# Reordering the beginning of a transformer-block kernel: tokens in column halves, modulation in chunks of 128 columns

## The chip, the cores and the metric

The kernel runs on one core of a Trainium2 chip. A core has five engines, each with its own in-order instruction stream: TensorE (PE in the profile; its weight loads are listed apart as PEld), VectorE (DVE), ScalarE (ACT), GpSimd (POOL) and SyncE (SP), which here only issues transfers. They share an on-chip memory of 128 partitions (SBUF); TensorE writes its results to accumulator banks (PSUM), of which this kernel uses eight, each of 128 x 512 fp32 values. The metric is device time in microseconds (us), the median of several runs; an arithmetic result in fp32 precision is wanted.

## The reference

One layer of a diffusion backbone, on 1024 latent tokens (a grid of 16 rows by 64 columns) and 256 context tokens of width 1024. What the change touches is its first two steps:

```
mod_x = silu(c) @ w_mod + b_mod                  # also for the context, with c_ctx
sh1, sc1, ... = split(mod_x, 6)
h_x = rmsnorm(x, g_pre_mix) * (1 + sc1) + sh1    # modulated tokens
u, q, k, v  = split(h_x @ w_in)                  # first 512 columns of w_in give u
```

After that come the pooling mixer, neighbourhood attention, an output projection and a squared-ReLU MLP. They are the same in both kernels.

## The kernel before, in words

**Precision.** A product of two fp32 matrices is made of three products in a faster format: each operand is split into a high part and the rest, a low part, and high x high, high x low and low x high are added up in one bank. ScalarE makes the high part (`high_part`, a rounding copy), VectorE the low part (`low_part`, a subtraction). For the weights w_in these are tiles `wu0h`, `wu0l` and so on, one pair for each 256 rows of K; for the tokens a page `hx`, whose first half is the high and whose second half the low part.

**The start.** All of it is recorded inside `in_order(...)`, which fixes the order of instructions on every engine to that of the program text. No scheduler moves anything: an instruction that waits holds up all that stands behind it on its engine.

1. SP issues the loads: eight tiles of 128 tokens (`token_tile`, 512 KB each), then for each of four quarters q of the columns the modulation weights (`mod_load`, four transfers of 512 KB, `wm`, which pick runs of 1 KB out of w_mod) and a weight block (`load`, 512 KB, `wu0w` to `wu3w`), then the context and further weights. At most eight transfers are outstanding: the ninth waits for the landing of the first, and so on.
2. Per token tile: ScalarE squares and sums (`mean_square`, L131), VectorE adds epsilon (L136, `vt_x`), POOL takes the inverse root (L140, `rt_x`), VectorE scales the tile (`normalised`, L334). In the program text the squares of tile n+1 and its epsilon add stand ahead of the scaling of tile n.
3. TensorE turns the scaled tiles (transposes, `turned`, L346) into PSUM banks `pxt`, 128 columns of K at a time, so that k = 0 to 7 counts chunks of 128 rows of K. `spare` (L341) fills with transposes of the identity. `by_bands` (L353) copies a bank to the page `xT[k]`, on ScalarE or VectorE, putting the tokens in the order of eight bands of 8 grid columns. Latent half b = 0 holds bands 0 to 3 and b = 1 bands 4 to 7, so each half needs all eight token tiles.
4. The modulation: for a quarter q, `mod_sums` (L401) makes 16 products of 256 columns with the activated vectors c and c_ctx as stationary operand, in four groups of 32 array columns; ScalarE copies the result (`mrow`, L406), two small products with a picking matrix (L418) turn it into columns, and VectorE makes scale a1 and shift s1 of two chunks k (`shift_scale`, L422 to L427).
5. `latent(b, k)` applies scale and shift to one half of chunk k and makes its high and low part: with `on_act` unset ScalarE writes the high part from xT (L208) and VectorE computes h again (L209) and subtracts (L210); with it set ScalarE computes h (L205), then the high part (L206).
6. `some_sums(b, js, k)` (L449) makes the wide products, 512 columns each, for output blocks js: 12 for b = 0 and four blocks, 6 for b = 1 and two.

The order before is: all eight tiles scaled and turned, first quarter of the modulation, then chunk by chunk the wide products, with the sums of the next quarter between them. Eight banks are shared: two of them (`lasting`) for the modulation and a few others, six for the rest.

Of the kernel before, what the change touches and what calls it, by code (L numbers as in the profile page):

```python
# [18 lines left out]
P = 128  # L19
# [5 lines left out]
GW = 64  # L25
# [44 lines left out]

def _pick_table():

    e = np.zeros((P, 4), np.float32)
    for w in range(2):
        for v in range(2):
            e[32 * w + v, 2 * w + v] = e[64 + 32 * w + v, 2 * w + v] = 1.0
    return e
# [3 lines left out]
def hybrid_block(ctx, tc, x, ctx_in, w_mod, b_mod, gp1, gp2, w_in, pool_w, rpb, w_out, w1, w2, vectors,  # L81
# [189 lines left out]
    with tc.tile_pool(name="ps1", bufs=6, space=PSUM) as ps1, tc.tile_pool(name="tmp1", bufs=3) as tmp:  # L271

        def bank(name):
            if name[:2] == "pm" or name in ("pxt1_0", "pxt0_2", "pxt1_7", "pct2", "pct3"):
                return lasting(name)
            return ps1.tile([P, 512], F32, tag="mm", name=name)
# [20 lines left out]
        def mod_load(q, kh, w):  # L297
            src = w_mod[:, w * D + q * 256 : w * D + (q + 1) * 256].rearrange("(h k p) f -> h p k f", p=P, h=2)
            t = page(f"wm{q}_{kh}_{w}")
            nc.sync.dma_start(t.rearrange("p (k f) -> p k f", k=4), src[kh])  # L300
            return t

        xn = [token_tile(f"x{n}", x[n * P : (n + 1) * P, :]) for n in range(NT)]
        wm, raw_u = [], []
        for q in range(4):
            wm.append([[mod_load(q, kh, w) for w in range(2)] for kh in range(2)])
            raw_u.append(load(f"wu{q}", pair(w_in, q, 0, 512)))
# [17 lines left out]
        inverse = {}  # L325

        def squares(name, t):
            jk = page(f"jk{name}")
            ms = sm(f"ms_{name}", 1, 4)
            mean_square(jk, t, ms)  # L330
            inverse[name] = rsqrt_of(f"t_{name}", ms)

        def normalised(name, t):
            nc.vector.tensor_scalar_mul(t, t, inverse[name])  # L334

        xT = [None] * KT

# [5 lines left out]
        def turned(pts, ns, ks):  # L343
            for k in ks:
                for n in ns:
                    nc.tensor.transpose(pts[k][:, (n % 4) * P : (n % 4 + 1) * P], xn[n][:, k * P : (k + 1) * P], ident)  # L346

        def by_bands(copy, h, ks):
            for k in ks:
                if xT[k] is None:  # L350
                    xT[k] = page(f"xT{k}")
                to = xT[k].rearrange("p (m r c) -> p m r c", m=NM, r=QR)[:, :, 8 * h : 8 * h + 8]
                copy(to, pts[h][k].rearrange("p (r m c) -> p m r c", m=NM, c=QC))  # L353


        on_act, on_dve = nc.scalar.copy, nc.vector.tensor_copy
        pts = [{}, {0: bank("pxt1_0")}]
        free = pts[1][0][:, 3 * P :]

        def turned_in(h, ns, ks):  # L360
            for k in ks:
                if k not in pts[h]:
                    pts[h][k] = bank(f"pxt{h}_{k}")
            turned(pts[h], ns, ks)

        spare(free, 30)
        squares("x0", xn[0])
        for n in range(NT):
            if n + 1 < NT:
                squares(f"x{n + 1}", xn[n + 1])  # L370
            if n == 5:
                by_bands(on_dve, 0, (0,))
            if n == 7:
                by_bands(on_dve, 0, (1,))
            normalised(f"x{n}", xn[n])
            if n < 4:
                turned_in(0, (n,), range(KT - 1))
        spare(free, 3)
        turned_in(1, (4,), (0,))
        spare(free, 10)  # L380
        turned_in(0, (0, 1, 2, 3), (7,))
        turned_in(1, (5,), (0,))
        spare(free, 3)
        by_bands(on_dve, 0, (2,))
        by_bands(on_act, 0, (3, 4, 5, 6, 7))
        turned_in(1, (4, 5), (4, 5))
        turned_in(1, (6,), (0, 4, 5))
        turned_in(1, (4, 5, 6), (1,))
        turned_in(1, (7,), (0, 1, 4, 5))
        turned_in(1, (4, 5, 6, 7), (6,))  # L390
# [5 lines left out]
        def mod_sums(q, pm, kh):  # L396
            for k in range(4 * kh, 4 * kh + 4):
                for w in range(2):
                    c = 2 * (k % 2) + w
                    o = (k % 4) * 256  # L400
                    nc.tensor.matmul(pm[32 * c : 32 * c + 32, :256], sT[:, k, :], wm[q][kh][w][:, o : o + 256],  # L401
                                     start=(k < 2), stop=(k >= KT - 2))

        def mod_kept(q, pm):
            mr = tmp.tile([P, 256], F32, tag="mrow", name=f"mrow{q}", bufs=2)
            nc.scalar.copy(mr, pm[:, :256])  # L406
            return mr
# [6 lines left out]

        def shift_scale(q, mr):
            pt = bank(f"pmt{q}")
            for j in range(2):
                nc.tensor.matmul(pt[:, 4 * j : 4 * j + 4], mr[:, j * P : (j + 1) * P], pck, start=True, stop=True)  # L418
            pv = pt[:, :8].rearrange("p (j w v) -> p w v j", w=2, v=2)
            hs = slice(2 * q, 2 * q + 2)  # L420
            for v in range(2):
                nc.vector.tensor_tensor(a1[v][:, hs], pv[:, 1, v], b_sc[:, hs], add)  # L422
                nc.vector.tensor_tensor(a1[v][:, hs], a1[v][:, hs], g1c[:, hs], mul)
                if q < 2:
                    nc.vector.tensor_tensor(s1[v][:, hs], pv[:, 0, v], b_sh[:, hs], add)
                else:
                    nc.vector.scalar_tensor_tensor(s1[v][:, hs], pv[:, 0, v], -1.0, b_sh[:, hs], mul, sub)  # L427
# [3 lines left out]
        def latent(b, k):  # L431
# [3 lines left out]
                      on_act=(b == 1), kept=src if b == 1 or k > 1 else None)  # L435
# [6 lines left out]
        pus = [[bank(f"pu{j}_{b}") for j in range(4 if b == 0 else 2)] for b in range(2)]  # L442

        def some_sums(b, js, k):
            h = hx[b][k]
# [17 lines left out]
        wu0h, wu0l = (whl.tile([P, 1024], F32R, tag="hl", name=f"wu0{n}") for n in "hl")  # L463
        by_bands(on_dve, 1, (0,))
        by_bands(on_act, 1, (1, 4, 5))
        by_bands(on_dve, 1, (6,))
        pm = bank("pm0")
        for kh in range(2):
            mod_sums(0, pm, kh)
        mr = mod_kept(0, pm)  # L470
        nc.scalar.copy(wu0h, raw_u[0])
        wgt.append((wu0h, wu0l))
        turned_in(1, (4, 5, 6, 7), (3,))
        shift_scale(0, mr)
        turned_in(1, (4, 5, 6, 7), (2, 7))
        nc.vector.tensor_tensor(wu0l, raw_u[0], wu0h.bitcast(F32), sub)
        latent(0, 0)
        latent(0, 1)
        by_bands(on_act, 1, (3, 2))
        by_bands(on_dve, 1, (7,))  # L480
        latent(1, 0)
        latent(1, 1)
        for q in range(4):
            some_sums(0, range(4), 2 * q)
            if q == 0:
                some_sums(0, (0, 1), 1)
            if q < 3:
                mr = mod_rows(q + 1)
                wgt.append(high_low(f"wu{q + 1}", raw_u[q + 1], 1.0 if q == 0 else -1.0))
            some_sums(0, range(2 if q == 0 else 0, 4), 2 * q + 1)  # L490
# [6 lines left out]
            if q == 2:  # L497
                for i, t in enumerate(cp):
                    squares(f"c{i}", t)
                for i, t in enumerate(cp):  # L500
                    normalised(f"c{i}", t)
# [46 lines left out]
        for k in range(2):  # L548
            hi, lo = hx[0][k][:, :512], hx[0][k][:, 512:]
# [1502 lines left out]
```

## Time and profile before

| | us |
|---|---|
| median of 3 runs (1027.5 to 1028.42) | 1027.59 |
| the profiled execution | 1028.11 |
| its span | 1026.3 |
| TensorE busy | 1012.1 |
| first wide product of the start | 23.18 |
| first product with the third weight block (wu2) | 45.01 |

Rows of a timeline give the start in us, the length in us, the engine, the line, the operation, out<-in, sizes and the count; in brackets the idle time of the engine before it and what ended it. Rows of waits give who waited for whom, us in total, times and the longest. Rows of a stretch give its length, then the busy time and the count for PE, PEld, DVE, ACT and POOL, the granted TensorE clock, the share of the transfer engines and GB/s. A matmul of fp32 operands shows as two records.

### The profile page before, as it was taken

The numbers are of one execution on the slowest core, as the hardware profiler recorded it, in microseconds if no ns is written. First come the engines' busy times: TensorE is split into PE (matmuls) and PEld (weight loads), VectorE is DVE, ScalarE is ACT, GpSimd is POOL, SyncE is SP. The second block draws the span as 40 slices with busy tenths as digits, with TensorE's granted clock in tenths as the row PEclk, the third lists the DMA queues.
The fourth block names the chain that finished last, engine by engine and source line by source line (L and its number), as shares of the span: only waits on it lengthen the run. The fifth ranks groups of instructions, "written<-read, shape, count | busy, mean of one in ns | idle before, by whom it ended". The sixth has DMA issues, their size and how long they took to land.

```text
span 1026.3 us, 16024 instructions
## 1 busy us (share of the span) xinstructions
PE 1012.1 (99%) x5910; PEld 839.0 (82%) x5910; DVE 746.8 (73%) x1156; ACT 546.0 (53%) x944; POOL 148.9 (15%) x230
## 2 busy tenths in 40 slices
PE   8999999999999999999999999999999999999997
PEld 6788888878898888888888888888888888888885
DVE  5588757977886688879998888755757666556576
ACT  7573254348896657776555554555543344334431
POOL 3011110156773321310000000000000000000001
PEclk9999999999999999999999999999999999999999
DMA  9999799623347966886776657537966766556556
GB/s 343 336 253 342 233 266 310 205 58 88 84 96 204 229 171 200 274 206 204 260 253 205 224 196 227 182 133 238 347 231 248 248 231 214 196 184 193 175 178 213
DMA packets 123134, 222.70 MB, mean 217 GB/s; under 512 B 9456, under 2 KB 55152, under 8 KB 123056
## 3 DMA queue, kind: packets, MB, share of 16 engines
q1 hardware_dynamic: 96560, 171.14, 50.7%
q0 software_dynamic: 9360, 19.58, 9.4%
q10 hardware_dynamic: 17136, 30.97, 8.1%
q8 instruction: 46, 0.75, 0.3%
q14 instruction: 32, 0.26, 0.1%
HBM read 168.16 MB, written 52.45 MB: 215 GB/s over the span
## 4 chain that ended last, share of the span: by engine, by line
PE 94%; DMA 2%; POOL 1%; ACT 1%; issue 1%; DVE 1%; SPq 0%; POOLq 0%; DVEq 0%; ACTq 0%
PE pu L449 4%; PE pa L1096 4%; PE phz L198 3%; PE phv L198 3%; PE pyx L198 3%; PE phx L198 3%; PE phx L200 3%; PE pyv L200 3%; PE pyx L200 3%; PE pyz L200 3%; PE pyv L199 3%; PE phz L199 3%; PE pyz L199 3%; PE phv L199 3%; PE phx L199 3%; PE phz L200 3%
## 5 line engine op out<-in xcount | busy, mean ns | idle before, releaser
L1042 ACT ACTIVATE sp<-sp,nm 128x640 f32<-128x640 f32 (+1 forms) x64 | 51.5, 805 | 9.6 <-DVE ri L1046 4.8
L1031 DVE CUSTOM_DVE_ANT_0 sp<-S,tab 128x640 f32<-128x640 f32 (+1 forms) x56 | 44.5, 794 | 14.1 <-PE pz L1062 10.3
L1638 ACT ACTIVATE c<-c 128x512 f32<-128x512 f32 x48 | 30.3, 631 | 45.9 <-DVE c L1758 25.7
L146 ACT CAST wpS<-S 128x512 fp32r<-128x512 f32 x64 | 38.8, 616 | 26.5 <-PE phv L200 9.9
L198 PE MATMUL phx<-thB,wpA 128*128 128x512 f32 x128 | 50.2, 392 | 0.0
L200 PE MATMUL phx<-thB,wpA 128*128 128x512 f32 x128 | 49.8, 389 | 0.0
L199 PE MATMUL phx<-tlB,wpA 128*128 128x512 f32 x128 | 49.8, 389 | 0.0
L152 DVE TENSOR_TENSOR wpS<-S,wpS 128x512 fp32r<-128x512 f32 x64 | 43.4, 685 | 7.6 <-ACT wpS L146 7.6
L140 POOL TENSOR_TENSOR ry<-vy,nhalf 128x1 f32<-128x1 f32 x8 | 5.9, 740 | 281.3 <-DVE vy L138 281.3
L1639 ACT ACTIVATE c<-c 128x512 f32<-128x512 f32 x48 | 30.3, 630 | 15.2 <-DVE sa L1721 12.1
L198 PEld LDWEIGHTS phx<-thB,wpA 128*128 128x128 f32 x128 | 24.0, 188 | 5.4 <-ACT s L1689 0.5
L200 PEld LDWEIGHTS phx<-thB,wpA 128*128 128x128 f32 x128 | 24.0, 188 | 5.0
L199 PEld LDWEIGHTS phx<-tlB,wpA 128*128 128x128 f32 x128 | 24.1, 188 | 4.8
L1081 DVE COPY pt<-T 128x512 f32<-128x512 f32 x32 | 21.9, 686 | 5.8 <-PE T L1062 5.8
L1096 PE MATMUL pa<-pt,v 128*64 128x128 f32 x352 | 25.9, 280 | 0.2
L198 PE MATMUL phz<-thB,wpS 128*128 128x512 f32 x64 | 25.0, 391 | 0.0
L198 PE MATMUL phv<-thT,wpA 128*128 128x512 f32 x64 | 25.0, 391 | 0.0
L199 PE MATMUL phz<-tlB,wpS 128*128 128x512 f32 x64 | 24.9, 390 | 0.0
L199 PE MATMUL phv<-tlT,wpA 128*128 128x512 f32 x64 | 24.9, 389 | 0.0
L200 PE MATMUL phz<-thT,wpS 128*128 128x512 f32 x64 | 24.9, 389 | 0.0
L200 PE MATMUL phz<-thB,wpS 128*128 128x512 f32 x64 | 24.9, 389 | 0.0
L200 PE MATMUL phv<-thT,wpA 128*128 128x512 f32 x64 | 24.9, 389 | 0.0
(1134 smaller groups left out, 3434.4 us busy)
## 6 DMA issues: line engine op xcount, KB each, us to landing
b<-in_w SPq DMA_DIRECT2D x64, 512.0 KB, 4.4
hrS<-hdS SPq DMA_DIRECT2D x32, 512.0 KB, 5.4
hrA<-hdA SPq DMA_DIRECT2D x24, 512.0 KB, 5.6
wm<-in_w_mod SPq DMA_DIRECT2D x16, 512.0 KB, 9.7
wa_0w<-in_w SPq DMA_DIRECT2D x16, 512.0 KB, 5.0
wa_1w<-in_w SPq DMA_DIRECT2D x16, 512.0 KB, 4.5
hdA<-c ACTq DMA_DIRECT2D x32, 256.0 KB, 2.9
hdS<-sa ACTq DMA_DIRECT2D x32, 256.0 KB, 3.2
```

The costliest lines, as they stand in the source:

```text
L146: nc.scalar.copy(hi, src)
L152: nc.vector.tensor_tensor(lo, src, hi.bitcast(F32), sub)
L198: nc.tensor.matmul(ps, ahi, bhi, start=first, stop=False, skip_group_check=more)
L199: nc.tensor.matmul(ps, ahi, blo, start=False, stop=False, skip_group_check=more)
L200: nc.tensor.matmul(ps, alo, bhi, start=False, stop=last, skip_group_check=more)
L449: nc.tensor.matmul(pus[b][j], wk(wgt, k, low, j * P, P), r, start=(k == 0 and n == 0), stop=(k == KT - 1 and n == 2))
L1031: nc.vector.tensor_tensor_reduce(out=to, in0=s, in1=bt, scale=1.0, scalar=BIG, op0=add, op1=ALU.min, accum_out=nm)
L1042: nc.scalar.activation(sp, sp, AF.Exp, bias=least[i, e], scale=-1.0, accum_out=sums[i][:, e : e + 1])
L1081: copy(turns[i].rearrange("p e i t -> p (e i) t")[:, :, h * HD : (h + 1) * HD], turned[i][h].rearrange("p (a t) -> p a t", a=8))
L1096: nc.tensor.matmul(pa[e * HD : (e + 1) * HD, cols], v[:, f : f + HD], turns[i][:, e, c] if c < 4 else fifths[i][:, :, (e + 1) * HD : (e + ...
L1638: nc.scalar.activation(r, src, AF.Relu)
L1639: nc.scalar.activation(r, r, AF.Square)
```

## The change

The first part of the program is rewritten.

- **Tokens by columns.** A token tile is now four grid rows by 32 grid columns. Tiles 0 to 3 hold all of latent half b = 0, tiles 4 to 7 all of b = 1.
- **Loads.** Tiles 0 to 3 first, then the first quarter's modulation and weight block, then tiles 4 to 7, then the second quarter and so on. The first two quarters come in pieces for one chunk k: two pages of modulation weights and a half weight block (256 KB) each. The host writes the modulation weights once more, as `mod_pages`, in which every page lies whole, 4 KB for each partition.
- **Modulation by chunk** for k = 0 to 3: `mod_sums` with 16 products of 128 columns, one pick, and `chunk_scale` for one k. Quarters 2 and 3 are as before.
- **Scaling.** Tile n's epsilon add now stands behind the scaling of tile n-1.
- **Order.** First half turned for k = 0 to 6; chunk 0; wide products of (b = 0, k = 0) and (0, 1) with chunk 1 between; then tiles 4 to 7 squared, scaled and turned through three banks `pxb` that hold two chunks each and are filled and emptied twice (two tiles at a time, 256 columns for each copy); chunk 2; then (1, 0), (1, 1), (0, 2), (1, 2), the third quarter, (0, 3), (1, 3). From `latents(2)` on the order is that of before.
- **Values kept.** For b = 0 and k = 0, 1 VectorE's h is now written over xT; so the two adds that made it again later are gone.

```
...
+        xn = token_tiles(0)
+        first_loads(0)
+        xn += token_tiles(1)
+        first_loads(1)
...
+        def first_loads(q):
+            raw_u[q] = wraw.tile([P, 1024], F32, tag="raw", name=f"wu{q}w")
+            for i in range(2):
+                for kh in range(2):
+                    wm[q][i][kh] = mod_load(q, i, kh)
+                nc.sync.dma_start(raw_u[q][:, i * 512 : (i + 1) * 512], w_in[(2 * q + i) * P : (2 * q + i + 1) * P, :512])
...
+        def normalised(n):
+            nc.vector.tensor_scalar_mul(xn[n], xn[n], rsqrt_of(f"t_x{n}", means[n]))
...
+        def chunk_scale(k, pt, v):
+            ks = slice(k, k + 1)
+            nc.vector.scalar_tensor_tensor(a1[v][:, ks], pt[:, 2 + v : 3 + v], b_sc[:, ks], g1c[:, ks], add, mul)
+            nc.vector.tensor_tensor(s1[v][:, ks], pt[:, v : v + 1], b_sh[:, ks], add)
...
-                      on_act=(b == 1), kept=src if b == 1 or k > 1 else None)
+                      on_act=(b == 1 and k > 1), kept=src)
...
+        squared(0)
+        for n in range(4):
+            if n < 3:
+                squared(n + 1)
+            normalised(n)
+            if n < 3:
+                first_turned(n, range(KT - 1))
+                spare(free, 2)
         for kh in range(2):
-            mod_sums(0, pm, kh)
+            mod_sums(0, whole[0], kh, 0)
+        mr = chunk_row(0)
+        first_turned(3, range(2))
+        picked(pt[0], mr, 0)
+        first_turned(3, range(2, KT - 1))
+        half_weight(0, 0, high_part)
+        by_bands(on_dve, pxt[0], 0, 0, 0)
+        chunk_scale(0, pt[0], 0)
         latent(0, 0)
+        by_bands(on_act, pxt[1], 1, 0, 0)
+        by_bands(on_act, pxt[3], 3, 0, 0)
+
+        half_weight(0, 0, low_part)
+        by_bands(on_dve, pxt[2], 2, 0, 0)
+        chunk_scale(0, pt[0], 1)
+        some_sums(0, (0, 1), 0)
+        chunk_sums(1, 0)
+        some_sums(0, (2, 3), 0)
+        chunk_sums(1, 1)
+        by_bands(on_act, pxt[4], 4, 0, 0)
+        by_bands(on_dve, pxt[5], 5, 0, 0)
+        mr = chunk_row(1)
+        half_weight(0, 1, high_part)
+        picked(pt[1], mr, 0)
+        chunk_scale(1, pt[1], 0)
+        half_weight(0, 1, low_part)
         latent(0, 1)
+        pxt[7] = bank("pxt7")
+        for n in range(4):
+            first_turned(n, (7,))
+        by_bands(on_dve, pxt[6], 6, 0, 0)
+        by_bands(on_dve, pxt[7], 7, 0, 0)
+        chunk_scale(1, pt[1], 1)
+        some_sums(0, range(4), 1)
+
+        pxb = [bank(f"pxb{i}") for i in range(3)]
+        two = lambda k: pxb[k // 2][:, (k % 2) * 256 : (k % 2 + 1) * 256]
...
+        for n in range(4, NT):
+            squared(n)
+        for n in (4, 5):
+            normalised(n)
+            second_turned(n, range(6))
+        chunk_sums(2, 0)
+        normalised(6)
+        banded(on_act, (0, 2, 3, 4), 0)
+        banded(on_dve, (1,), 0)
+        second_turned(6, range(4))
+        chunk_sums(2, 1)
+        normalised(7)
+        banded(on_dve, (5,), 0)
+        second_turned(7, range(4))
+        for n in (6, 7):
+            second_turned(n, (4, 5))
+        mr = chunk_row(2)
+        banded(on_act, (0,), 8)
+        banded(on_dve, (1,), 8)
+        picked(pt[2], mr, 0)
+        chunk_scale(2, pt[2], 0)
         latent(1, 0)
         latent(1, 1)
-        for q in range(4):
+        half_weight(1, 0, high_part)
+        half_weight(1, 0, low_part)
+        pus[1] += [bank(f"pu{j}_1") for j in range(2)]
+        banded(on_act, (2,), 8)
+        banded(on_dve, (3,), 8)
+        latent(0, 2)
+        chunk_scale(2, pt[2], 1)
+        some_sums(1, range(2), 0)
+        banded(on_act, (4,), 8)
+        banded(on_dve, (5,), 8)
+        last_chunk(6)
+        for kh in range(2):
+            chunk_sums(3, kh)
+        mr = chunk_row(3)
+        half_weight(1, 1, high_part)
+        half_weight(1, 1, low_part)
+        some_sums(1, range(2), 1)
+        picked(pt[3], mr, 0)
+        for v in range(2):
+            chunk_scale(3, pt[3], v)
+        latent(1, 2)
+        some_sums(0, range(4), 2)
+        last_chunk(7)
+        latent(0, 3)
+        latent(1, 3)
+        some_sums(1, range(2), 2)
+        mr = mod_rows(2)
+        wgt.append(high_low("wu2", raw_u[2], -1.0))
+        some_sums(0, range(4), 3)
+        shift_scale(2, mr)
+        some_sums(1, range(2), 3)
+        latents(2)
+        for q in (2, 3):
             some_sums(0, range(4), 2 * q)
...
-        for k in range(2):
-            hi, lo = hx[0][k][:, :512], hx[0][k][:, 512:]
-            nc.vector.tensor_tensor(xT[k][:, :512], hi.bitcast(F32), lo.bitcast(F32), add)
...
```

`first_turned`, `second_turned` and `last_chunk` transpose tiles of the first half, of the second half for k up to 5, and of the second half for one k; `half_weight` makes the high or low part of one half weight block; `banded` calls `by_bands` on half a bank.

191 lines of the change are left out of this document (94 added, 97 removed).

## The prediction

> **What bounds the kernel now.** I read the page's first lines, then who waited for whom on TensorE, then its timeline for the first 48 us, then the busy time of three stretches (length, then TensorE's busy time).
>
> ```profile
> span 1026.3 us, 16024 instructions
> PE 1012.1 (99%) x5910; PEld 839.0 (82%) x5910; DVE 746.8 (73%) x1156; ACT 546.0 (53%) x944; POOL 148.9 (15%) x230
> ```
>
> ```profile
> PE pa L1062 <- POOL rb L1048: 1.8, 3, 0.8
> PE pxt L346 <- DVE x L334: 1.7, 4, 0.8
> PE pu L449 <- ACT hx L208: 0.4, 1, 0.4
> PE S L1016 <- DVE nm L1031: 0.3, 1, 0.3
> ```
>
> ```profile
> 1.57 5.72 PE L341 MATMUL pxt<-ident 128*128 128x128 f32 x30 [1.57 <-POOL ident masks.py:199]
> 8.07 0.98 PE L346 MATMUL pxt<-ident,x 128*128 128x128 f32 x7 [0.77 <-DVE x L334]
> 16.39 2.18 PE L346 MATMUL pxt<-ident,x 128*128 128x128 f32 x18 [0.69 <-DVE xT L353]
> 23.18 1.21 PE L449 MATMUL pu<-hx,wu0h 128*128 128x512 f32 x4 [0.43 <-ACT hx L208]
> 37.08 1.94 PE L401 MATMUL pm<-wm,sT 128*32 128x256 f32 x32
> 39.98 1.07 PE L449 MATMUL pu<-hx,wu1l 128*128 128x512 f32 x4
> 40.88 1.08 PE L449 MATMUL pu<-hx,wu1h 128*128 128x512 f32 x4
> 45.01 1.07 PE L449 MATMUL pu<-hx,wu2h 128*128 128x512 f32 x4
> ```
>
> ```profile
> 31.22 0.34 PE pmt L418 x4
> ```
>
> ```profile
> 23.18:45.01 21.83, 21.83 (x144) 16.39 (x145) 13.48 (x31) 13.33 (x20) 0.00 (x0) 1.00 1.08 362
> ```
>
> ```profile
> 0.00:23.18 23.18, 18.82 (x147) 15.62 (x147) 12.22 (x38) 16.65 (x30) 7.90 (x15) 1.00 0.97 342
> 23.18:1010.00 986.82, 984.24 (x5725) 816.20 (x5726) 727.15 (x1108) 527.93 (x911) 139.31 (x212) 1.00 0.68 215
> ```
>
> TensorE is idle for 14.2 of 1026.3 us: 4.4 ahead of 23.18, where the wide products (`some_sums`, L449) begin, 2.6 from there to 1010, the rest at the very end. From there to 45.01, the first product with the third weight block wu2, it is busy 21.83 of 21.83 us. (The short row before these stretches is from the chain that ended last: two picks of the modulation's columns, 0.17 each.) So only TensorE's own sequence up to 45.01 matters: when it reaches that product decides the end, since from there on the changed kernel has the same TensorE instructions in the same order, and no wait behind it exceeds 0.8 us (the first row of waits, at L1062). The profiled execution took 1028.11 us, 1.8 more than its span and 0.5 more than the median, 1027.59; I take the difference found below and add it to the median.
>
> **The change, part by part.** Times below are us from the span's start.
>
> *Loads.* SP issues 33 transfers where it issued 31, all before it first waits for a weight buffer.
>
> ```profile
> DMA to landing us min/median/max: 3.9/6.7/8.8
> 0.74 4.43 SPq L293 DMA_DIRECT2D x<-in_x  x8
> 3.72 8.59 DMA x<-in_x
> 10.00:11.00 1.00, 0.71 (x7) 0.47 (x6) 0.51 (x1) 0.98 (x2) 0.91 (x1) 1.00 1.02 410
> 16.00:17.00 1.00, 0.61 (x6) 0.61 (x7) 1.00 (x3) 1.00 (x3) 0.14 (x1) 1.00 1.10 349
> ```
>
> The first token tile lands at 0.74 + 3.9 = 4.6, the seventh at 3.72 + 8.59 = 12.3: 1.28 each, at 410 GB/s. Modulation tiles, in runs of 1 KB, came at 349 GB/s, 1.5 each; laid out whole, with 4 KB per partition as the tokens have, I price them at 1.28 too, and a half weight (256 KB) at 0.7. Then tokens 0 to 3 land by 8.5, the first chunk's two pages at 9.7 and 11.0, its half weight at 11.7, the second chunk's at 13.0, 14.3 and 14.9, tokens 4 to 7 from 16.2 to 20.1, the third chunk's pages at 21.3 and 22.6, the last page at 38. Below, TensorE needs these at 11.9, 17.9, 22 and 28.8: the new order of loads is hidden with 1 us to spare or more. Were pages still 1.5 each, the last would land 4 later, still early.
>
> *First half of the tokens.* Steps between engines go by these rows.
>
> ```profile
> 6.13 0.15 DVE L136 TENSOR_SCALAR vt_x<-ms_x 128x1 f32<-128x1 f32 x1
> 6.37 0.55 POOL L140 TENSOR_TENSOR rt_x<-vt_x,nhalf 128x1 f32<-128x1 f32 x1 [4.86 <-DVE vt_x L136]
> 7.26 0.75 DVE L334 TENSOR_SCALAR x<-x,rt_x 128x1024 f32<-128x1024 f32 x1
> 14.24 0.74 DVE L334 TENSOR_SCALAR x<-x,rt_x 128x1024 f32<-128x1024 f32 x1
> 14.90 0.15 DVE L136 TENSOR_SCALAR vt_x<-ms_x 128x1 f32<-128x1 f32 x1
> 15.65 0.68 DVE L353 COPY xT<-pxt 128x512 f32<-128x512 f32 x1
> 16.25 0.74 DVE L334 TENSOR_SCALAR x<-x,rt_x 128x1024 f32<-128x1024 f32 x1
> ```
>
> ```profile
> 20.78 0.37 ACT L406 COPY mrow<-pm 128x256 f32<-128x256 f32 x1 [1.27 <-PE pm L401]
> 21.05 1.05 ACT L471 CAST wu0h<-wu0w 128x1024 fp32r<-128x1024 f32 x1
> 22.31 1.52 ACT L208 ACTIVATE hx<-xT,s,a 128x512 fp32r<-128x512 f32 x2 [0.21 <-DVE s L425]
> 14.77 2.51 ACT L353 COPY xT<-pxt 128x512 f32<-128x512 f32 x5
> 58.75 1.04 ACT L131 ACTIVATE jkc<-c 128x1024 f32<-128x1024 f32 x1
> 22.53 1.21 DVE L476 TENSOR_TENSOR wu0l<-wu0w,wu0h 128x1024 fp32r<-128x1024 f32 x1
> 23.66 0.54 DVE L209 TENSOR_SCALAR hx_0t<-xT,a,s 128x512 f32<-128x512 f32 x1
> 24.30 0.69 DVE L210 TENSOR_TENSOR hx<-hx_0t,hx 128x512 fp32r<-128x512 f32 x1
> 24.91 0.54 DVE L209 TENSOR_SCALAR hx_1t<-xT,a,s 128x512 f32<-128x512 f32 x1
> ```
>
> In `normalised` the epsilon add (vt) of a tile now stands behind the scaling of the tile before. One tile is then a closed ring: scaling to vt 0.66 (14.24 to 14.90), vt to root 0.24, root 0.55, 0.06 to the next scaling: 1.5 per tile. The first scaling can start at 6.98, so the four start at 6.98, 8.5, 10.0 and 11.5; a scaling reaches TensorE 0.81 later (7.26 to 8.07). The third tile's seven transposes end at 11.6, two fillers at 11.9. Then comes the first chunk's sum: sixteen products of 128 columns where a quarter had sixteen of 256 (1.94). I take half, 0.95, as it is the columns that stream; if the price is per instruction, it is 1.94. That gives 12.9; row copy, 0.3 (0.37 for twice the columns), and pick with both handovers, 0.5, to 13.7; the copy of xT0 on VectorE till 13.9; scale and shift till 14.1; ScalarE's `hx` at 14.1; and 0.87 behind it (22.31 to 23.18) the first wide product, at 15.0 instead of 23.2. A head start of 8.2.
>
> *What TensorE has left.* Up to wu2: 72 wide products, 0.228 each (39.98 to 40.88 for four, and a little for the rest), 16.4; 36 transposes still to do at 0.12 (16.39: 2.18 for 18), 4.4; three chunks 2.9; one quarter 1.9; five picks of 0.17, 0.9. Together 26.5, and 0.13 for a restart after a wait (the four at 23.18 took 1.21, later ones 1.07 or 1.08), on about five of the ten below, 0.65. Without waits it reaches wu2 at 42.1, a gain of 2.9. That is all the change can bring: 4.4 of transposes and half the modulation now stand behind the first product.
>
> *The waits that it adds.* Each engine keeps its written order, so I follow the four in step.
> 1. The low weight half stands on VectorE behind `latent(0, 0)`, whose h now overwrites xT0 and so waits for ScalarE's read: done 14.9, h 0.64, low 0.61, weight half 0.69: 16.9. TensorE needs it at 15.4 (it issues one product in between): wait 1.6.
> 2. Then six wide products, a page and four more to 20.2; row, pick, scale 1.2, `hx` and 0.87: 22.3. TensorE has only the k=7 transposes till 21.5: 0.8.
> 3. Twelve products end at 25.1. VectorE, from 22.3: h and low of hx1, copies of xT6 and xT7 (0.6 each), four small steps: vt of tile 4 only at 24.9, scaling at 25.8, TensorE at 26.6: 1.5. ScalarE's squares (1.05 apart, from 22.2) and the landed tiles are ready.
> 4. to 7. Ring by ring, 1.5 each against six transposes (0.7): tile 5 at 28.1, 0.8; tile 6 needs k=1's copy out of its bank, behind the scaling: 29.9 for 29.3, 0.6; tile 7 at 31.5 for 30.8, 0.6; hx of the second half, behind tile 7's copy: 33.2 for 32.6, 0.6.
> 8. The second accumulator of `some_sums(1, range(2), 0)` takes the bank of chunks 2 and 3 of the second tokens; its last reader, the copy of xT3, stands on VectorE behind two h and two low parts (from 33.2: 0.64 + 0.61 + 0.64 + 0.61) and the low half of wu1 (0.61), and takes 0.35 itself: 36.7. TensorE, one product on, stood at 33.5: 3.3. Behind it queue all later products.
> 9. to 10. The bank for k=6, 0.3; scale to `hx` at wu2, where only six products cover what twelve covered, 0.3.
>
> Sum 10.4. TensorE then reaches wu2 at 15.0 + 26.5 + 0.65 + 10.4 = 52.55 for 45.0: 7.5 later.
>
> *Hidden.* Two adds that remade xT0 and xT1 go from VectorE, about 1.4, but TensorE waits for VectorE nowhere behind 45 by more than 0.3. POOL does the same roots, later, ahead of its transfers of combined weights; these and SP's wk2 and wk3, held by the low parts of wu2 and wu3, move with TensorE. The relayout of pages costs the chip nothing.
>
> *Bounds.* A chunk at full price adds 1.0 on each of three chunks and the first, less 1.0 that waits 4 to 7 absorb: up to 3. The 256-column copy on VectorE is not in the trace: between a small step, 0.15, and 0.68; 0.35, half a copy, is nearest by ScalarE's 0.37 for that size; three on the path, -0.6 to +1. A root beside a scaling took longer here (0.94 and more by most rows), but in the ring none runs beside one: 0 to +2. If VectorE's steps overlap better, waits 1 to 7 shrink by a third: -2.
>
> One rule speaks to the waits. The thirty fillers took 0.19 each (5.72), later transposes 0.12: the array began slow, and no idle stretch long enough to make it slow again is in this trace. The Trainium skill (TensorE: Matmul & The Clock Gate, What's actually happening) says that a fully idle window of about 3.4 us halves the clock until some 3.4 us of work. By that rule my longest wait, 3.3, just escapes.
>
> **The rivals.**
> - *The clock falls at wait 8.* Thirty fillers at 0.19 against 0.12 cost 2.1; the wait has only to grow a little. 1035.1 + 2.1 = 1037.2. This is what the Trainium skill's rule above would make of a slightly longer wait.
> - *Chunks cost by instruction.* Weights are loaded as often as before for half the columns. 1038.1. Against it: sixteen products (32 records) in 1.94 are streams of 256 columns.
> - *Wait 8 is short,* if VectorE is not late there: 3.3 less, 1031.8. Against it: five steps of known length stand ahead.
> - *The head start holds: faster.* The place is VectorE between 15 and 37; if its work ran so far ahead that the ten waits summed to under 2.9, the kernel would win, at best 1024.7. For it: VectorE was busy only 13.48 of 21.83 us in that stretch. Against it: a ring of 1.5 per tile is latency, not load.
> - *Nothing shows:* waits of just 2.9, 1027.6.
>
> **How the numbers follow.** Forecast 1027.6 + 7.5 = 1035.1, chance 0.58 with its own range 1032.5 to 1036.7. Clock 0.07, chunks 0.13, wait 8 short 0.12: all slower, together 0.90. Faster 0.06, no change within 0.2% (2 us, about what the measurement tells apart) 0.04. The range, 1031 to 1040, leaves out the last two and the tails of two causes together.
>
> **What would show it.** The first L447 product near 15 us and the first with wu2h near 52.5; in the list of waits of TensorE new entries for VectorE's scaling (L377), about 3 us in three or four times, and one of about 3 us for the copy of xT at `by_bands` (L367) ahead of `pu`; a page of eight 128-column products in about 0.5. No wait on `wm` or `x` transfers. I am wrong if wu2h comes before 47, or if TensorE waits for a page.

## The result, and the profile after

The changed kernel took 1071.66 us (1071.46 to 1072.34) where the kernel before took 1027.55 on the same chip: a ratio of 1.043, 95% interval 1.0417 to 1.0443. Forecast were 1035.1 us, range 1031 to 1040. The direction was right; the size was not, by 37 us, and the range did not hold it.

The profiled execution took 1071.46 us with a span of 1069.7. From its page, the span, TensorE's busy time, and in 40 slices TensorE's busy tenths, its clock and the share of the transfer engines:

```profile
span 1069.7 us, 16149 instructions
PE 1024.3 (96%) x5964; PEld 846.7 (79%) x5964; DVE 749.4 (70%) x1166; ACT 544.8 (51%) x948; POOL 146.7 (14%) x230
PE   3759999999999999999999999999999999999997
PEclk6669999999999999999999999999999999999999
DMA  5584979882433897688677648635886765546557
```

All the loss is in the first three or four slices (26.7 us each): TensorE is a third busy in the first, at a mean clock of 0.6 in three. Its list of waits, and rows of its timeline:

```profile
PE pxt L360 <- DVE x L377: 15.4, 3, 5.8
PE pm L393 <- DMA wm<-in_mod_pages: 11.8, 3, 10.1
PE pu L447 <- DVE xT L367: 3.1, 1, 3.1
PE pxb L360 <- DVE x L377: 2.2, 2, 1.3
```

```profile
19.54 1.75 PE L360 MATMUL pxt<-ident,x 128*128 128x128 f32 x7 [4.73 <-DVE x L377]
27.48 1.76 PE L360 MATMUL pxt<-ident,x 128*128 128x128 f32 x7 [5.76 <-DVE x L377]
35.77 1.27 PE L447 MATMUL pu<-hx,wu0h 128*128 128x512 f32 x2
62.88 1.08 PE L393 MATMUL pm<-wm,sT 128*32 128x128 f32 x16 [10.12 <-DMA wm<-in_mod_pages]
71.82 0.67 PE L447 MATMUL pu<-hx,wu0h 128*128 128x512 f32 x1 [3.08 <-DVE xT L367]
89.16 1.19 PE L447 MATMUL pu<-hx,wu2h 128*128 128x512 f32 x4
```

The first wide product starts at 35.77 (forecast 15.0) and the first with wu2 at 89.16 (forecast 52.55; 45.01 before). That is 44.2 later than before, and the span is 43.4 longer: as forecast, all is decided by then. Two entries of the list were not in the forecast at all. The scaling is named for 15.4, but VectorE was not late. ScalarE's squares wait in turn for the token tiles:

```profile
L144 ACT ACTIVATE jkx<-x 128x1024 f32<-128x1024 f32 x8 | 8.4, 1055 | 37.0 <-DMA x<-in_x 37.0
wm<-in_mod_pages SPq DMA_DIRECT2D x16, 512.0 KB, 20.0
```

Two stretches of the same trace (the last two columns are the share of the sixteen transfer engines and GB/s) show what the tiles are late for. While one is loaded, the share is that of a quarter of the engines, and nearly all the time just four packets of 4 KB are under way at once:

```profile
5.00:10.00 5.00, 2.76 (x16) 2.52 (x14) 0.00 (x0) 0.19 (x1) 0.00 (x0) 1.00 0.25 102
25.00:30.00 5.00, 2.18 (x9) 1.78 (x9) 0.91 (x2) 0.90 (x3) 0.55 (x1) 0.50 0.26 103
```

So there were three questions: why the tiles come at a quarter of the pace, what the slow clock costs, and whether the ten waits of the forecast are there once the loads are not.

### The profile page after: what moved, and what is told of

Its sections match the earlier page's. It is cut to its first block, busy times and chain, and to the rows that moved or that the text cites. A ratio compares the mean times of both kernels' runs of the same rounds, so it can differ in the third digit from the quotient of the medians.

```text
span 1069.7 us, 16149 instructions
## 1 busy us (share of the span) xinstructions
PE 1024.3 (96%) x5964; PEld 846.7 (79%) x5964; DVE 749.4 (70%) x1166; ACT 544.8 (51%) x948; POOL 146.7 (14%) x230
## 4 chain that ended last, share of the span: by engine, by line
PE 91%; DMA 5%; SPq 2%; POOL 1%; issue 0%; ACT 0%; DVE 0%; DVEq 0%; POOLq 0%; ACTq 0%
PE pu L447 4%; PE pa L1212 3%; PE phx L211 3%; PE phz L211 3%; PE pyx L211 3%; PE phv L211 3%; PE pyv L213 3%; PE phv L212 3%; PE phz L212 3%; PE pyz L213 3%; PE pyz L211 3%; PE pyv L211 3%; PE phx L213 3%; PE pyx L212 3%; PE phx L212 3%; PE phz L213 3%
## 5 line engine op out<-in xcount | busy, mean ns | idle before, releaser
L1754 ACT ACTIVATE c<-c 128x512 f32<-128x512 f32 x48 | 30.3, 631 | 43.4 <-DVE c L1874 25.4
L144 ACT ACTIVATE jkx<-x 128x1024 f32<-128x1024 f32 x8 | 8.4, 1055 | 37.0 <-DMA x<-in_x 37.0
L211 PE MATMUL phv<-thT,wpA 128*128 128x512 f32 x64 | 25.0, 391 | 0.0
L211 PE MATMUL phy<-thT,wpS 128*128 128x512 f32 x64 | 24.9, 389 | 0.0
```

The source lines that it names most:

```text
L211: nc.tensor.matmul(ps, ahi, bhi, start=first, stop=False, skip_group_check=more)
L1754: nc.scalar.activation(r, src, AF.Relu)
```

## The experiments: the loads

**Whole tiles.** The changed kernel, with token tiles that the host has laid out as eight blocks of 128 rows.

```
-  token_tile(f"x{n}", grid[4*(n%4) : 4*(n%4)+4, 32*b : 32*b+32])
+  token_tile(f"x{n}", x_tiles[n])
```

> The changed kernel, but the host lays the eight token tiles out whole, so that a tile is one transfer of 128 rows of 4 KB; order, tokens and all else unchanged. Theory A (a tile of 4 by 32 rows keeps only 4 of 16 transfer engines busy, and nearly all of the loss is that): token tiles land about 1.3 us apart, the share of busy transfer engines is about 1.0 instead of 0.25, the first wide product comes near 15 us, the first product with wu2h near 52.5, and the time is 1035 (1033 to 1038), that is slower than before by the ten waits forecast. Theory B (the new order or the slow array clock is what costs, the transfers are only late because their waiting places come free late): the time stays above 1060. Theory C (no loss is left once the transfers are right): 1025 to 1028.

Measured: 1040.13 us (1038.25 to 1040.33), ratio 1.0107 (1.0091 to 1.0124). The first wide product starts at 15.56, the first with wu2 at 57.85 in place of 89.16. The shape of the token loads, with all that follows from it, is 31.5 of the 44 us. The time lies 2 above the range that was expected (1033 to 1038), so something else costs about 5; the section on the clock is about that.

**Four transfers for each tile**, each of 32 rows that lie side by side.

```
+  for r in range(4):
+      nc.sync.dma_start(t[32*r : 32*r+32, :], grid[4*(n%4) + r, 32*b : 32*b+32])
```

> The changed kernel, but each token tile is loaded by four transfers of 32 adjoining rows, from the same places of the tokens. Theory A (how many engines one transfer is spread over): 32 rows spread over all engines, so the tiles land at a rate near the issuing one, four issues of about 0.45 us for a tile; first wide product at 15 to 17 us, time 1035 to 1040. Rival D (the places are slow to read, rows of a tile lie 256 KB apart): as slow as the changed kernel, 1065 to 1075.

Measured: 1040.78 us in one run. The same rows from the same four places, named in four transfers, give a kernel as fast as that with whole tiles. So the distance of the places is not what cost the 30 us. The loads themselves are slower than whole tiles, though:

```profile
6.00:11.00 5.00, 3.88 (x26) 3.41 (x25) 1.82 (x4) 2.64 (x6) 1.10 (x2) 1.00 1.05 225
```

All engines are busy (1.05), but they move 225 GB/s and not 410, and the first wide product starts at 17.32 instead of 15.56. Why these transfers of 128 KB are slow stays open. That the kernel ends no later is luck: in this execution the clock, treated below, fell at other places.

**The same shape in the kernel before,** 4 by 32 and 8 by 16.

```
-  xn = [token_tile(f"x{n}", x[n*P : (n+1)*P, :]) for n in range(NT)]
+  xn = [token_tile(f"x{n}", grid[4*(n%4) : 4*(n%4)+4, 32*(n//4) : 32*(n//4)+32]) for n in range(NT)]
```

> The kernel before with one thing of the change: its eight token loads take four grid rows by 32 columns each, as the changed kernel's do; all else as before, so the tokens come in another order than its copies assume and the output is permuted. Theory A: the eight tiles come at about 105 GB/s, 5 us each, 40 us for all instead of 10, with the modulation queued behind: wide products begin at 48 to 55 us instead of 23, time 1052 to 1060. Theory B (order and clock): 1027 to 1030.

> As the run before it, but each load takes eight grid rows by 16 columns (output permuted too). Theory A (as many engines as the outermost count of the pattern allows): 8 of 16 engines, a share of 0.5 and about 210 GB/s, 2.5 us for a tile, 20 us for all: wide products begin near 33 us, time 1036 to 1040, between the two. Rival D (places that lie far apart are slow): as the run with 4 by 32 or worse, since the pieces are smaller.

Measured: 1062.86 and 1045.66 us, one run each. The stretch from 15 to 20 us of the one, then two stretches of the other:

```profile
15.00:20.00 5.00, 1.76 (x7) 1.36 (x7) 0.83 (x2) 1.13 (x3) 1.01 (x1) 0.50 0.26 105
```

```profile
5.00:10.00 5.00, 2.25 (x16) 2.01 (x14) 0.15 (x1) 1.15 (x2) 0.55 (x1) 0.95 0.52 146
15.00:20.00 5.00, 1.76 (x7) 1.36 (x7) 1.23 (x4) 2.30 (x4) 1.17 (x2) 0.50 0.51 194
```

Four blocks give a share of 0.26 and 105 GB/s, eight 0.51 or 0.52 and 146 to 194: up to about 25 GB/s for each block. The share goes with the count; why the eight moved fewer bytes in the first stretch stays open. Both ended above the range that was expected, by 3 and by 6: I had priced the loads alone, and the array clock fell to a half in both (the column ahead of the share).

**The same places, columns as the outer index.** 32 columns of 4 rows name the same 128 rows.

```
+  grid = x.rearrange("(r w) d -> w r d", w=GW)
+  xn = [token_tile(f"x{n}", grid[32*(n//4) : 32*(n//4)+32, 4*(n%4) : 4*(n%4)+4]) for n in range(NT)]
```

> The kernel before, with each token tile loaded as 32 columns of 4 grid rows: the same 128 rows of 4 KB, at the same places in memory as a tile of the changed kernel, but named with the column as the outer of the two indices (the tokens come to lie in another order, so it computes another arrangement of them). Theory, that the count of the outermost index decides how many transfer engines share a transfer (4 gave a share of 0.25, 8 gave 0.5): 32 gives all sixteen, share 1.0, tiles 1.3 us apart, 1027.6. Rival, that rows from distant places are slow: share 0.25, 1063 as with 4 by 32.

Measured: 1029.76 us in one run, and all transfer engines at work (in the second row the modulation weights are already under way):

```profile
5.00:10.00 5.00, 3.38 (x23) 2.90 (x21) 0.99 (x3) 2.42 (x5) 1.57 (x2) 1.00 1.01 383
11.00:16.00 5.00, 3.98 (x22) 3.62 (x23) 3.18 (x7) 4.50 (x8) 3.90 (x4) 0.72 1.05 385
```

It ended 2 above the expectation: ScalarE's squares of the third tile, which wait for its landing, began 3.6 behind those of the second in this execution, the others 1.3 to 1.4 apart, and the clock fell for one stretch (0.72 in the second row). Why that tile was late stays open.

**The changed kernel, columns outer.** The same in the change itself, with a transpose that writes its columns back in the order of rows.

```
-  nc.tensor.transpose(to, xn[n][:, k*P : (k+1)*P], ident)
+  nc.tensor.transpose(to.rearrange("p (r c) -> p c r", r=4), xn[n][:, k*P : (k+1)*P], ident)
```

> The changed kernel with its token tiles loaded with the column as the outer index (32 columns of 4 rows), nothing laid out anew by the host; each transpose writes its 128 columns in the order of rows again, so that all behind it stays as it is. Theory of the count: tiles land 1.3 apart, and the time is that of the kernel with whole tiles, 1040.1 (1038 to 1042). If a transpose that writes with a stride costs more, each of the 64 adds to it: doubled, 64 times 0.11 is 7, of which about half is hidden, 1043. Rival, distant places: 1070.

Measured: 1039.35 us (1038.44 to 1040.32), ratio 1.0106 (1.0091 to 1.0121). The tokens are not laid out anew, and what whole tiles gave is there. Seven transposes at full clock take 0.98 us in this trace too, as in the kernel before: the stride costs nothing.

So it is the count of the outermost index, as the transfer names it: with 4 the share is 0.25, with 8 it is 0.5, with 32 it is 1. The packets of 4 KB under way at once say the same: 4, 8 and 16 nearly all the time. The Trainium skill says this in DMA: Bandwidth & Descriptors (Why a DMA increments its semaphore by 16 and not by 1): the number of engines is the largest up to 16 that divides the size of the slowest index on both sides. The shares above agree with it.

**Pages alone.** The kernel before with only its modulation pages laid out whole.

```
-  nc.sync.dma_start(t.rearrange("p (k f) -> p k f", k=4), src[kh])
+  nc.sync.dma_start(t, mod_pages[4*q + 2*kh + w])
```

> The kernel before with only its modulation pages laid out whole by the host (4 KB for each partition in place of four runs of 1 KB), everything else in the order of before. Theory: pages land 1.28 apart in place of 1.5, nothing waits for them: no change, 1027.6 (1026.6 to 1028.6). Rival, that the relayout itself costs or gains on the chip: over 1029.6 or under 1025.5.

Measured: 1027.84 us, ratio 0.9996 (0.9986 to 1.0006). This part of the change costs and brings nothing.

## The experiments: the clock

With whole tiles the time was still 5 above the forecast. Three stretches of that trace (length, TensorE's busy time, ..., clock):

```profile
13.28:16.69 3.41, 2.52 (x19) 1.32 (x11) 1.99 (x5) 2.78 (x6) 0.00 (x0) 1.00 1.04 411
16.69:20.10 3.41, 2.62 (x16) 1.75 (x20) 2.12 (x6) 0.26 (x1) 0.00 (x0) 0.50 1.02 411
20.10:23.52 3.42, 3.42 (x22) 2.02 (x16) 0.00 (x0) 0.00 (x0) 0.00 (x0) 0.50 1.03 405
```

The clock is at a half from 16.69 to 23.52 and again from 40.58 to 44.00, and no idle stretch of TensorE ahead of either is longer than 2.9 us. In all the traces, leaving out the first 5 to 8 us and the last 5 to 7, the times at half clock are multiples of 3.41 us (in the changed kernel's 30.7, 17.1 and 3.4). That led to a theory: every 3.41 us the clock is set by how much TensorE worked in the last such stretch.

Where the borders of these stretches lie differs from trace to trace: the first rise to full clock comes between 4.9 and 7.6. So the clock falls at other places under the same order of work: with four transfers for each tile at 31.53 and 38.36, with columns outer at 29.34 and 39.58, and in neither near 16.7.

**Fillers.** Whole tiles, with 40 transposes of the identity in three gaps.

```
+  spare(free, 6)                                    # ahead of the first product
+  spare(free, 8)                                    # inside some_sums(0, (0, 1), 0)
+  spare(whole[2][:, 128:256], 26)                   # inside some_sums(1, range(2), 0)
```

> The kernel with token tiles laid out whole (1040.1), plus 40 transposes of the identity as fillers in three gaps of TensorE: 6 behind the last tile of the first half, 8 ahead of the first product with the low weight half, 26 between the first two products of the second latent half, which wait for the copy of xT3. Nothing else is moved. Theory: the array clock is set anew every 3.41 us from the share of the last such stretch in which TensorE worked, and falls when that is under about half; no fully idle stretch is needed. Then the fillers keep it at 1.0, the products from 17.5 to 23.5 and from 40.6 to 44.0 run at full speed and 5.1 us come back: 1035.0 (1034 to 1036.5), the first product with wu2h near 52.8. Rival: the slow clock only filled time in which TensorE would have waited anyway; then 1038 to 1040. Rival: the clock falls only after a fully idle stretch and something else made these products slow; then the fillers change nothing, 1040.

Measured: 1047.25 us, ratio 1.0186 (1.0169 to 1.0203): 7 slower instead of 5 faster. The row of the 26:

```profile
44.04 4.77 PE L361 MATMUL pm<-ident 128*128 128x128 f32 x26 [4.31 <-DVE s L427]
```

I had put them into the bank of the modulation, in columns that nothing reads. But the program orders the accesses to this bank though they touch other columns: the fillers waited 4.3 us for VectorE's last read of it, for the scale of chunk 2, which stands far back on VectorE. It was no test of the theory; a filler needs a bank that is free.

**Work thrown away, in free places.**

```
+  spare(pus[0][0][:, :P], 7)                        # bank of the first sum, ahead of its first product
+  again 4 times: the second product of (b = 0, k = 0)
+  again 11 times: the first product of (b = 1, k = 0), while the next waits for xT3
```

> The kernel with whole tiles (1040.1), with work that is thrown away in three gaps of TensorE, and this time in places that nothing reads: 7 transposes of the identity into the bank of the first accumulator before its first product, the second product of the first block four times more (it starts its sum anew, so only the last counts), the first product of the second latent half eleven times more while the next one waits for the copy of xT3. Theory of stretches of 3.41 us: each stretch is then over half busy, the clock stays at 1.0 from 7 us on, and the 5.1 us come back, 1035.0 (1034 to 1036.5), the first product with wu2h near 52.8. Rival: the slow clock only filled waits: 1038 to 1040.

Measured: 1036.16 us (1035.95 to 1036.35), ratio 1.0076 (1.0061 to 1.0091). The clock is 1.0 from 7.2 us on. Fifteen useless products and seven useless transposes make the kernel 4.0 faster than whole tiles without them.

**The kernel before without its 16 fillers** behind the first half bank.

```
-  spare(free, 3)
-  spare(free, 10)
-  spare(free, 3)
```

> The kernel before without the 16 fillers that stand behind the first half bank (3, 10 and 3); nothing waits for them, and no idle stretch of TensorE becomes longer than about 1.5 us. Theory of stretches of 3.41 us with a limit of about half: between 12.7 and 16.4 only six transposes are left, 0.7 us of work; the clock falls to a half for one stretch, 17 transposes and the first modulation quarter take 1.7 longer, less a wait of 0.4 that this fills: first wide product near 24.5, 1029.0 (1028.3 to 1029.5). Rival, that only a fully idle stretch of 3.4 us lowers the clock: no change, 1027.6.

Measured: 1029.74 us (1028.08 to 1030.32), ratio 1.0013 (1.0003 to 1.0022). It is 1.5 more than the 1028.22 of the kernel before on the same chip, where 1.4 was expected; the ten runs scatter by 2.2. The profiled one:

```profile
13.98:17.39 3.41, 1.78 (x12) 1.35 (x13) 3.41 (x7) 3.41 (x7) 1.48 (x2) 1.00 1.10 348
17.39:20.80 3.41, 3.41 (x25) 2.62 (x27) 1.80 (x3) 1.67 (x4) 0.00 (x0) 0.50 1.08 363
```

```profile
16.60 3.39 PE L346 MATMUL pxt<-ident,x 128*128 128x128 f32 x18 [1.00 <-DVE xT L353]
24.80 1.19 PE L446 MATMUL pu<-hx,wu0h 128*128 128x512 f32 x4 [0.50 <-ACT hx L208]
```

A stretch with twelve transposes, in which the longest idle time is 1.00, is followed by one at half clock: eighteen transposes take 3.39 instead of 2.18, and the wide products start 1.6 later (24.5 was expected). So no fully idle stretch is needed. The Trainium skill (TensorE: Matmul & The Clock Gate, What's actually happening) speaks of a free-running window and of an idle window that lowers the clock; the grid of 3.41 agrees with the first, these rows do not agree with the second. Where the limit lies the traces show only roughly: a stretch shown busy for 0.52 of its length fell (above), so did one of 0.54 (fillers, from 37.35); others of 0.51 (the last run below), 0.57 (early copies, below) and 0.61 (work thrown away) did not, and the one of 2.52 in 3.41 with whole tiles fell; the ends of matmuls are modelled, and its last two wide products are drawn out to 0.96 where two take 0.46.

## The experiments: the waits

**Early copies.** Whole tiles, the first two groups of the unlucky fillers, and the copies of xT2 and xT3 directly behind those of xT0 and xT1.

```
   banded(on_dve, (1,), 8)
+  banded(on_act, (2,), 8)
+  banded(on_dve, (3,), 8)
```

> As the last, with the 6 and 8 fillers but without the 26; instead the two copies of xT2 and xT3 (second half of the bank that the second accumulator takes over) stand directly behind those of xT0 and xT1, ahead of the two latents and the weight half on ScalarE and VectorE. Theory: the wait of 2.9 us (my wait 8) is VectorE's written order alone; it shrinks to under 0.5, the hx of the second half comes 0.4 later, and the low part of hx is waited for by about 0.8 instead: 1035.0 less 1.7, 1033.3 (1032.3 to 1034.5). Rival: the bank is held by something else, then 1035 or, with the clock falling again, 1037.

Measured: 1042.2 us, ratio 1.0132 (1.0117 to 1.0147); 8.9 above the expected 1033.3. The fillers took 2.9 (they held the scale of chunk 0 for 1.15, and waited themselves for 1.7), the clock fell for two stretches of 3.41, and a new wait stands behind the old one:

```profile
38.85 0.73 PE L453 MATMUL pu<-hx,wu0h 128*128 128x512 f32 x2 [0.67 <-ACT hx L226]
43.42 1.09 PE L364 MATMUL pxb<-ident,x 128*128 128x128 f32 x4 [2.52 <-DVE s L427]
```

The first two products of the second half now follow each other: wait 8 was VectorE's written order, as the forecast said. But the next transposes need the bank that the same late scale still reads, 2.5.

**Early tokens.** The last, with tiles 4 and 5 squared and scaled while TensorE is at the second chunk, and the epsilon adds of 6 and 7 one scaling earlier.

```
   by_bands(on_dve, pxt[5], 5, 0, 0)
+  squared(4)
+  squared(5)
+  rooted(4)     # epsilon add and root
+  scaled(4)
+  rooted(5)
```

> As the last; besides, tiles 4 and 5 are squared and scaled while TensorE is at the second chunk and the first wide products (VectorE and ScalarE stand idle there for 6 us), and the epsilon add of tiles 6 and 7 stands ahead of the scaling before it, as in the kernel before. Theory: waits 3 to 7 (1.3, 0.6, 0.4 and 0.3 in the trace of the kernel with whole tiles) are the ring of VectorE and POOL; 1.5 to 2.3 of them go: 1031.3 (1030 to 1032.5). That would still be slower than the kernel before, 1027.6: what is left is wait 1, the handovers row to pick to scale to hx of chunks 1 and 2, and handovers to hx. Rival: TensorE is then held by hx and scale, which hide the gain: 1033.

Measured: 1039.32 us, ratio 1.0109 (1.0094 to 1.0124). 2.9 less than the last, where 2.0 was expected: of waits 3 to 6 only 0.2 is left in TensorE's list. The level stayed 8 above the expected 1031.3, by the same fillers, the wait of 2.5 and the clock.

**All of it, with no filler in a bank that is read.** Also the low part of the first half weight ahead of VectorE's part of the first latent, and both scales of chunk 2 together.

```
   chunk_scale(0, pt[0], 0)
+  half_weight(0, 0, low_part)
   latent(0, 0)
...
-  chunk_scale(2, pt[2], 0)
+  for v in range(2):
+      chunk_scale(2, pt[2], v)
```

> The kernel with whole tiles and every wait shortened that the runs have shown: low part of the first half weight ahead of VectorE's part of the first latent, copies of xT2 and xT3 early, tiles 4 and 5 squared and scaled early, the epsilon adds of 6 and 7 early, both scales of chunk 2 together (the wait of 2.5 for the second of them took the place of my wait 8), and 7 transposes of fill before the first product. Theory: of the run with early tokens (1039.3) go the delay of 1.15 and the wait of 1.7 that its fillers made themselves, wait 1 (0.9), the wait of 2.5, and both falls of the clock, 3: 1030 (1028.5 to 1031.5); still slower than the kernel before, as handovers (row to pick to scale to hx, three times 0.7 to 0.8) and the first product at 15.4 leave under 3 us to win. Rival: under 1027.0, a version that beats both; rival: a new wait of VectorE in the second half of the tokens, 1032 to 1034.

Measured: 1030.78 us, ratio 1.0025 (1.0015 to 1.0035), where 1030 was expected. TensorE's main waits between the first wide product and wu2 in the profiled run, which took 1032.56:

```profile
PE pu L462 <- ACT hx L226: 1.5, 2, 0.8
PE pm L420 <- ACT mrow L410: 1.2, 1, 1.2
PE pm L406 <- ACT xT L371: 0.7, 1, 0.7
```

**And more of it:** the squares of tile 5 behind the row copy of chunk 1, the copy of xT6 early, four transposes of tile 4 in the wait for hx.

```
-  squared(5)
...
   latent(0, 1)
+  for n in (5, 6, 7):
+      squared(n)
...
+  second_turned(4, (0, 1, 4, 5))
```

> The reordered kernel (1030.8), with the squares of tile 5 behind the row copy of chunk 1 instead of ahead of it, the copy of xT6 early, and four of tile 4's transposes in the wait for hx of chunk 1. Theory: the wait of 1.2 for the row falls to 0.4, the wait of 0.8 for hx to 0.4, the stretch from 20.5 to 23.9 is over half busy and the clock no longer falls in any run: 1.2 to 2.9 less, 1028.9 (1027.5 to 1030). That is about the kernel before and no better: 3 us of transposes and modulation still lie behind the first product, and the handovers stay. Rival: the waits move to the scaling of tile 5, 1031.

Measured: 1030.82 us (1030.65 to 1031.05), ratio 1.0024 (1.0014 to 1.0033): nothing gained, where 1028.9 was expected.

```profile
PE pu L462 <- ACT hx L226: 1.0, 2, 0.7
PE pxb L364 <- DVE xT L371: 0.7, 1, 0.7
PE pm L406 <- ACT xT L371: 0.7, 1, 0.7
PE pm L420 <- ACT mrow L410: 0.4, 1, 0.4
```

The two waits shrank as expected (1.2 to 0.4, and hx by 0.5), but a copy of VectorE's took 0.7 of it back, and in this execution the first wide product came 0.35 later (15.78 for 15.43). The time is that of the rival, but the wait that the rival names, for the scaling of tile 5, is only 0.2. The fall of the clock (in the profiled run before, from 23.92 to 27.33) went too. But only two of the eight runs of that kernel had it, by their times (1032.3 and 1032.6, the others 1030.1 to 1030.9), so the median had little to gain. No version here beats the kernel before.

## Why the prediction was right in its direction and wrong in its size

The two runs that take one cause each divide the delay of the first wu2 product:

| | wu2 at | |
|---|---|---|
| kernel before | 45.01 | |
| loads and clock taken away (work thrown away) | 53.60 | order: +8.6, forecast 7.5 |
| loads taken away (whole tiles) | 57.85 | clock: +4.3, forecast 0 |
| changed kernel | 89.16 | loads: +31.3, forecast 0 |

The 31.3 holds the clock that starved products brought with them; it isn't divided further. Of the 4.3, 0.3 lie ahead of the first wide product; the first fall of the clock cost 2.7 (8.88 for 6.22 from that product to the columns of the second chunk), the second 1.3 (4.34 for 3.03 behind wait 8).

**The step that failed: *Loads*.** "Then tokens 0 to 3 land by 8.5 ... the new order of loads is hidden with 1 us to spare or more." I took the pace of 1.28 from tiles of 128 adjoining rows and kept it for tiles that the change names as 4 by 32. Tile size and run length had stayed the same, so I saw no new price; the outermost count had gone from 128 to 4, and with it sixteen engines to four, 105 GB/s for 410. I looked for a bound only for the pages (1.5 for 1.28). The pages, and all else that is queued behind, came late too: the "no wait on `wm` or `x` transfers" became 27 us of TensorE's waits.

**The clock.** I named it, and only at wait 8, on the belief that a fully idle 3.4 us is needed; chance 0.07, price 2.1. It fell twice in the kernel with whole tiles, the first time near 16.7 among waits below 1 us, and cost 4.0 (1040.1 to 1036.2). Where it falls differs by execution (above), so the 4.0 is no fixed price. What failed is that sentence of the forecast, and with it the fixed prices of 0.228 for a product and 0.12 for a transpose behind a thin stretch.

**The steps that held,** in the run with work thrown away, where neither of the two disturbs:

```profile
15.25 0.50 PE L453 MATMUL pu<-hx,wu0h 128*128 128x512 f32 x1
17.16 0.73 PE L453 MATMUL pu<-hx,wu0l 128*128 128x512 f32 x2
21.47 0.39 PE L411 MATMUL pm<-cols,mrow 128*128 128x4 f32 x2 [0.39 <-ACT mrow L401]
23.13 1.19 PE L453 MATMUL pu<-hx,wu0h 128*128 128x512 f32 x4 [0.78 <-ACT hx L226]
27.47 0.84 PE L364 MATMUL pxb<-ident,x 128*128 128x128 f32 x6 [1.32 <-DVE vt_x L154]
34.09 2.79 PE L452 MATMUL pu<-hx,wu0h 128*128 128x512 f32 x11 [0.53 <-ACT hx L226]
37.52 0.50 PE L453 MATMUL pu<-hx,wu0h 128*128 128x512 f32 x1 [0.41 <-DVE xT L371]
53.60 1.20 PE L453 MATMUL pu<-hx,wu2h 128*128 128x512 f32 x4
```

- Head start: first wide product at 15.25, forecast 15.0.
- Wait 1: two products from 15.25 would end at 15.7, the low weight half comes at 17.16: 1.4, forecast 1.6.
- Wait 2: 0.39 and 0.78, forecast 0.8. Wait 3: 1.32, forecast 1.5.
- Waits 4 to 7: 0.61, 0.43, 0.32 and 0.53, forecast 2.6, measured 1.9.
- Wait 8: the first product could have been followed at 34.3, and was at 37.52: 3.2, forecast 3.3; 3.08 in the changed kernel. Waits 9 and 10, forecast 0.6, are not there.
- The waits sum to 9.0, forecast 10.4. What TensorE had to do itself takes 53.60 - 15.25 - 9.0 = 29.4, forecast 27.15. This term, *What TensorE has left*, was too small by 2.2: a chunk takes about 1.15 with its changes of operand (18.29 to 18.86 for half of one), not 0.95, and the first four wide products behind a change take 1.04 (23.13 to 24.17), not 0.91.
- The chunk rival is out: sixteen products of 128 columns are nearer to half a quarter's price than to all of it.

So none of the rivals gives the measured time. The first did come true as an event: behind wait 8 the clock fell, at 40.58 with whole tiles and at 71.98 in the changed kernel, though the wait was no longer than forecast (2.9 and 3.1), and with whole tiles it cost 1.3 where 2.1 was priced. "The head start holds: faster" is told apart too: even with every wait shortened that the traces showed, the kernel ends 2.5 above the one before. The forecast's reason holds, and more strongly than it said: 4.4 us of transposes and half the modulation only move behind the first product. With the measured 29.4 a kernel without any wait would reach wu2 at 15.25 + 29.4 = 44.65, for 45.01 before. So about 0.4 us were to be won, not 2.9; this is an estimate from the terms above.

## What to carry to other kernels

When a change alters how a transfer names its rows, read the outermost count before the bytes: a pace read from one shape isn't the price of another, and swapping two indices was worth 30 us here. A wait names the last releaser (here VectorE's scaling), so follow the chain to the engine that stood idle for a transfer. A head start gained by moving work behind it is worth only the idle time that it fills. And thin stretches of a few microseconds on TensorE cost twice, by the wait and by the clock behind it.

## What was not expected of the hardware

- A transfer of 4 by 32 rows of 4 KB ran at 102 to 105 GB/s and a share of 0.25, one of 8 by 16 at 146 to 194 and 0.51 to 0.52, one of 32 by 4 at 383 and 1.01, from the same memory. Four transfers of 32 adjoining rows each ran at 1.05 too, but at 225 GB/s.
- The clock fell (0.50 in the row from 17.39 to 20.80) behind a stretch of 3.41 us in which TensorE worked for 0.52 of the time, with no idle time over 1.0 us; fifteen useless products and seven transposes made a kernel 4.0 us faster.
